# Block products of a feed-forward layer with three accumulator tiles, and token sums dealt out between pieces of a plain tile

## The chip, the cores and the metric

One core of a Trainium2 chip runs the whole kernel. The metric is the device time of one execution in microseconds (us), taken on that core; several executions are timed and their median counts. A profile is one further execution, recorded by the hardware profiler. The engines are named as in the profile: PE is TensorE (matmuls), PEld its weight loads, DVE is VectorE, ACT is ScalarE, POOL is GpSimd, SP issues the DMAs.

## The reference

Two trunk layers over 128 context tokens and 512 latent tokens, 1024 channels. Each layer has a mixer of three branches and a gated feed-forward part of width 2816. The change concerns the feed-forward part of the second layer:

```python
xf = rmsnorm(h, p['norm_ffn'][l]) * (1 + sc_f) + sh_f
gu = xf @ p['ffn_w_in'][l]
h = h + g_f * ((jax.nn.silu(gu[..., :D_FF]) * gu[..., D_FF:]) @ p['ffn_w_out'][l])
```

## The kernel before, in words

All 640 tokens are held with channels on the 128 partitions and tokens along the free axis, in two halves of 320 tokens (`HF`). Every fp32 operand is split into a high part in fp32r (`xh`, `wh`, `ah`) and the rest (`xl`, `wl`, `al`), and each product is three matmuls: high by high, low by high, high by low.

Weights come in tiles of 128 output channels: `fg0` to `fg21` are the gate's columns, `fu0` to `fu21` the up projection's, `fo` the output projection's. A tile's 1024 input channels are loaded in two pieces of 512 (`wr`, three buffers); ACT copies a piece to `wh` (L505, three buffers), and POOL (L509) or, for block products, DVE (L507) subtracts to `wl`. A plain tile is 8 x 2 x 3 = 96 matmuls of 128x320 (`mm_k`, L554), in one accumulator tile of two PSUM banks, one bank for each half of the tokens (`psg`, L428, three buffers). `Stream` (L288) keeps the list of all these units of work; `step` emits one block of input channels, and `ahead` loads and splits the weights of the next units.

In the second layer most gate and up tiles are not plain. `NPL = (22, 2)` (L32) says that of 22 tiles 22 are plain in the first layer and 2 in the second; the other 20 are **pairs**: `fg` and `fu` of the same number, taken as a 2x2 block matrix (gate and up by two halves of the input channels) times the 2x2 blocks of the input (two halves of the channels by two halves of the tokens). Seven products in place of eight give the four result blocks. A product is 4 x 3 = 12 matmuls (`mm_block`, L546). Its weight operand is a block or a sum of blocks (`ws`, on DVE, L534), its input operand a block of `xh`, `xl` or one of the token sums `xeh`, `xel`.

The seven products of a pair add up in one PSUM tile: products 1, 6, 7 and 4 in its bank 0, product 2 in bank 1, and after that products 5 and 3 in bank 1 (`PRODS`, L280; the last entry says whether a product starts a sum). Between them the partial sums are read out: `snap` (L1576, tile `sn`) copies bank 0 after products 1, 6 and 7, on ACT; `c11` (L1588, into `th`) reads bank 1 after product 2, `c22` (L1592, into `su`) after product 5, `c12` (L1595, into `th`) after product 3, and `mul` (L1602, L1603) reads bank 0 after product 4, all on DVE. The products of neighbouring pairs are interleaved: with q the present pair and n the next, the order on PE is q.6, q.5, q.7, n.1, q.4, n.2, q.3, then n.6 and so on. From the first pair on, these instructions keep the order in which they are written (`o`, L486). After each group of tiles (0 to 7, 8 to 14, 15 to 21) the eight output tiles `fo` follow as plain ones.

Ahead of this part stands `join` (L764) with the end of the output projection `wo7`, the norm and the modulated input, and then `token_sums` (L728): for each of four channel blocks k it adds the shift to the tiles `us` of k and k + 4 (ACT, L733, two pieces a tile, 128 and 512 tokens), makes four differences on DVE (L736 into `xt1`, L737 to L739 into `tsum`), copies `tsum` to `xeh` (ACT, L740) and subtracts to `xel` (DVE, L741). The order of these instructions, and of the weight splits written after them, is a scheduler's, by the order in which they are written and by readiness.

Of the kernel before, what the change touches and what calls it, by code (L numbers as in the profile page):

```python
# [18 lines left out]
P = 128  # L19
# [5 lines left out]
HF = T // 2  # L25
# [3 lines left out]
EPS = 1e-6  # L29
QL, KL, RD = 256, 128, 32  # L30
GROUPS = (((0, 11), (11, 22)), ((0, 8), (8, 15), (15, 22)))
NPL = (22, 2)  # L32

O_MQ, O_CKV, O_KR = 0, 256, 384
O_GQ, O_GK, O_GV, O_GR, O_GLR = 416, 672, 928, 1440, 1952
# [248 lines left out]
def mark(s):  # L284
    pass


class Stream:  # L288


    def __init__(self, load, split, psum, mm, mmb, ring):
        self.load, self.split, self.psum, self.mm, self.mmb, self.ring = load, split, psum, mm, mmb, ring
        self.subs, self.units, self.uses = [], [], []
        self.seen = {}
        self.done = set()
        self.posts = {}
        self.ps = {}
        self.raw = {}
        self.w = {}
        self.u = self.k = 0  # L300
        self.debt = 0.0
# [45 lines left out]
    def step(self):  # L347
        u = self.units[self.u]
        name, i, k0, kn, xs, c, last = (u[n] for n in ("name", "i", "k0", "kn", "xs", "c", "last"))
        if self.k == 0:  # L350
            first, then = u["pre"] if isinstance(u["pre"], tuple) else (u["pre"], None)
            if first:
                first()
            self.ahead()
            if then:
                then()
            if name not in self.ps:
                self.ps[name] = self.psum()
        k = self.k
        if u["prod"]:  # L360
            self.mmb(self.ps[name][:, c, :HF], self.w[i], k, xs, u["start"] and k == 0, k == kn - 1)
        else:
            self.mm(self.ps[name], self.w[i], k, k0 + k, xs, k0 + k == 0, last and k == kn - 1, c)
        self.k += 1
        if self.k == kn:
            self.k = 0
            self.u += 1
            self.uses[i] -= 1
            if self.uses[i] == 0:
                del self.w[i]  # L370
            if u["prod"]:
                if last:
                    self.done.add(name)
            elif last and (u["ph"] or c in (None, 1)):
                ps = self.ps[name] if c == 0 else self.ps.pop(name)
                ps = ps[:, :, :HF]
                with self.prio("pp"):
                    if u["ph"]:
                        self.posts[name](ps, c)
                    else:  # L380
                        self.posts.pop(name)(ps)
                if c != 0:
                    self.done.add(name)
                else:
                    self.done.add(name + "/0")
        return 0.82 if c is None else 0.41

    def steps(self, n):
        for _ in range(n):
            self.step()  # L390

    def fill(self, us):
        self.debt += us
        while self.debt > 0 and self.ready():
            self.debt -= self.step()
# [8 lines left out]
def tile_hybrid(ctx: ExitStack, tc, a):  # L404
# [11 lines left out]
    def pool(name, side, bufs=1):  # L416
        return tc.tile_pool(name=name, bufs=bufs, side=side, reuse_waits="tile")
# [10 lines left out]
    def psg(name):  # L428
        return ps2.tile([P, 2, 512], F32, name=name, tag="g")

    def psb(shape, name):
        return ps1.tile(shape, F32, name=name, tag="b")
# [79 lines left out]
    class Pair:  # L512


        def __init__(self, name, top, low):
            self.name, self.t, self.f = name, {}, int(name[2:].split(".")[0])
            self.src = {"A11": top[:, 0:512], "A12": top[:, 512:1024], "A21": low[:, 0:512], "A22": low[:, 512:1024]}
# [196 lines left out]
    def modulate_in(hs, us, rs, sc, sh, c, ds):  # L714
        for d in ds:
            t = us[d]
            if d < 7:
                (ge if OPT["mx"] >> d & 1 else ve).tensor_tensor(t[:, HS[c]], t[:, HS[c]], rs[:, HS[c]], op=ALU.mult)  # L718
            else:
                for i, s, e in PIECES[c]:  # L720
                    ve.scalar_tensor_tensor(t[:, s:e], hs[d][:, s:e], sc[:, d, i:i + 1], rs[:, s:e], op0=ALU.mult, op1=ALU.mult)
            for i, s, e in PIECES[c]:
                se.activation(xh[:, d, s:e], t[:, s:e], AF.Identity, bias=sh[:, d, i:i + 1])  # L723
            for i, s, e in PIECES[c]:
                ve.scalar_tensor_tensor(xl[:, d, s:e], t[:, s:e], sh[:, d, i:i + 1], xh[:, d, s:e], op0=ALU.add,  # L725
                                        op1=ALU.subtract)

    def token_sums(us, sh, xeh, xel, xt1, pool_):  # L728
        h0, h1 = HS
        for k in range(4):  # L730
            for d in (k, k + 4):
                for i, s, e in ((0, 0, TP), (1, TP, T)):
                    se.activation(us[d][:, s:e], us[d][:, s:e], AF.Identity, bias=sh[:, d, i:i + 1])  # L733
            u, v, t1 = us[k], us[k + 4], xt1[:, k]
            t = pool_.tile([P, 3, HF], F32, name="tsum", tag="tsum", bufs=2)
            ve.tensor_tensor(t1, u[:, h1], u[:, h0], op=ALU.subtract)  # L736
            ve.tensor_tensor(t[:, 0], v[:, h1], t1, op=ALU.subtract)  # L737
            ve.tensor_tensor(t[:, 1], v[:, h1], u[:, h1], op=ALU.subtract)
            ve.tensor_tensor(t[:, 2], v[:, h0], t[:, 0], op=ALU.subtract)  # L739
            se.activation(xeh[:, k], t, AF.Copy)  # L740
            ve.tensor_tensor(xel[:, k], t, xeh[:, k], op=ALU.subtract)  # L741
# [7 lines left out]
    def resid_posts(names, hs, g, nm, keep=False):  # L749
        def post(ps, c=None, d=0):  # L750
            if d < 7:
                h_update(hs, d, ps, g)
                nm.add(d, hs[d])
                if keep:
                    dma(hsp[d], hs[d])
            else:
                h_update(hs, d, ps, g, (c,))
                nm.end(hs[d], c)
                if keep:
                    dma(hsp[d][:, HS[c]], hs[d][:, HS[c]])  # L760
        for d in range(8):
            G.posts[names[d]] = lambda ps, c=None, d=d: post(ps, c, d)

    def join(name, hs, nm, after, pre=None):  # L764

        if pre:
            pre()
        G.to(name + "/0")
        G.steps(5)
        nm.fin(0)  # L770
        G.to(name)
        after(0, range(4))
        nm.fin(1)
        after(0, range(4, 8))
        after(1, range(8))
# [101 lines left out]
    def pair_l2(p, B, gp, keep, l):  # L877
        G.to(f"dq{p}.{l}")
        if OPT["l2"] == 0:
            l2_finish(p, ("dk",), B, gp, keep)  # L880
            fill(f"l2a{p}")
        G.to(f"dv{p}.{l}")
        fill(f"l2b{p}")
        l2_finish(p, ("dq",) if OPT["l2"] == 0 else ("dk", "dq"), B, gp, keep)
# [664 lines left out]
    class Blocks:  # L1549
# [21 lines left out]
            ve.tensor_tensor(xl[:, 0:4, h1], self.xt1, xh[:, 0:4, h1], op=ALU.subtract)  # L1571

        def ps(self, q, bank):
            return G.ps[q.name][:, bank, :HF]

        def snap(self, q, i):  # L1576
            t = self.s[q.name, i] = self.sn.tile([P, HF], F32, name="sn", tag="sn", bufs=4)
# [35 lines left out]
    def mm_any(ps, w, kw, kx, xs, start, stop, half):  # L1613
        mm_k(ps, w, kw, kx, cur[xs[0]] if isinstance(xs[0], str) else xs, start, stop, half)

    G = Stream(wload, wsplit, lambda: psg("gm"), mm_any, mm_block, 3)
    G.prio = prio

    def job(name, src, kt, xs, halves=None, ks=None, pre=None):
# [6 lines left out]
    for l in range(L):  # L1626
        def k8(n, halves=None, ks=None, l=l, pre=None):
            job(f"{n}.{l}", a["wall"][l, TILES[n]], 8, xs8, halves, ks, pre)
# [35 lines left out]
        for d in range(8):  # L1664
            k8(f"wo{d}", "post" if d == 7 else None)
        gr, npl = GROUPS[l], NPL[l]
        pairs = {f: Pair(f"ff{f}.{l}", a["wall"][l, TILES[f"fg{f}"]], a["wall"][l, TILES[f"fu{f}"]]) for f in range(npl, NF)}
# [6 lines left out]
        for gi, (f0, f1) in enumerate(gr):  # L1674
# [18 lines left out]
            for i, q in enumerate(qs):  # L1693
                r = qs[i - 1] if i else None
                ahead = (qs[i + 1:] + later + [None, None])[:2]
                n, n2 = ahead
# [25 lines left out]
    def fill(name):  # L1722
        G.fill(FILL[f"{name}@{cur['l']}"])
# [70 lines left out]
    for l in range(L):  # L1794
        prm, mod = prms[l], mods[l]
# [106 lines left out]
        with pool("gt", "right", 2) as gt:  # L1902
# [11 lines left out]
            with pool("zs", "left") as zs:  # L1914
# [6 lines left out]
                with pool("bd", "left") as bd, pool("kp", "left") as kp:  # L1921
# [11 lines left out]
                    for p in range(4):  # L1933
# [3 lines left out]
                        while late and f"br1_7.{l}" in G.done:  # L1937
                            q = late.pop(0)
# [30 lines left out]
        mark(f"normf{l}")  # L1969
        gr, npl = GROUPS[l], NPL[l]  # L1970
        if npl < NF:
            xctx = pool("xe", "left")
            F = Blocks(xctx.__enter__(), hs)
            with pool("us", "left") as up:
                us = [up.tile([P, T], F32, name=f"us{d}") for d in range(8)]
                join(f"wo7.{l}", hs, nm, lambda c, ds: modulate_in(hs, us, nm.acc, mod[:, 32:40], mod[:, 24:32], c, ds),
                     lambda: prescale(us, hs, mod[:, 32:40]))
                token_sums(us, mod[:, 24:32], F.xeh, F.xel, F.xt1, up)
        else:
            with pool("us", "left") as up:  # L1980
                us = [up.tile([P, T], F32, name=f"us{d}") for d in range(7)]
                join(f"wo7.{l}", hs, nm, lambda c, ds: modulate(hs, nm.acc, mod[:, 32:40], mod[:, 24:32], c, ds, us),
                     lambda: prescale(us, hs, mod[:, 32:40]))
# [105 lines left out]
```

## Time and profile before

| | |
|---|---|
| Median of 3 runs | 2898.85 us (2898.72 to 2901.0) |
| The profiled execution's own time | 2900.5 us |
| its span | 2898.7 us |
| mean granted clock of PE in it | 0.967 of full speed |
| PE busy | 2696.4 us (93%) |
| DVE, ACT, POOL busy | 1704.1, 1293.2, 1061.6 us |
| DMA | 317.10 MB, mean 109 GB/s |

How to read it: the profiled execution has its own time; its span is what the trace covers, and a change is summed against that execution. A row of the timeline gives the start from the beginning of the span, the time that it lasts, the engine, the line, the operation, output and inputs by the program's names, and how many equal ones are merged. A bracket at its end is the idle time of the engine before it and what ended that. Matmuls overlap in the pipeline: one lasts about 0.31 us, and the next starts about 0.147 us after it.

### The profile page before, as it was taken

The numbers are of one execution on the slowest core, as the hardware profiler recorded it, in microseconds if no ns is written. First come the engines' busy times: TensorE is split into PE (matmuls) and PEld (weight loads), VectorE is DVE, ScalarE is ACT, GpSimd is POOL, SyncE is SP. The second block draws the span as 40 slices with busy tenths as digits, with TensorE's granted clock in tenths as the row PEclk, the third lists the DMA queues.
The fourth block names the chain that finished last, engine by engine and source line by source line (L and its number), as shares of the span: only waits on it lengthen the run. The fifth ranks groups of instructions, "written<-read, shape, count | busy, mean of one in ns | idle before, by whom it ended". The sixth has DMA issues, their size and how long they took to land. (4 is left out here: it accounts for less than half of the span.)

```text
span 2898.7 us, 49712 instructions
## 1 busy us (share of the span) xinstructions
PE 2696.4 (93%) x19204; PEld 2464.4 (85%) x19204; DVE 1704.1 (59%) x3156; ACT 1293.2 (45%) x2438; POOL 1061.6 (37%) x772
## 2 busy tenths in 40 slices
PE   6889999889999999999999899988999998999998
PEld 4788888778879899999988888876877897898987
DVE  4765584747655699177358576566333336737373
ACT  5575655543333522122366555655233345424244
POOL 3543222333325467366445423233323352020203
PEclk9999999989999999999999999998999998999999
DMA  6254433345434355244323534332434231222222
GB/s 207 90 161 141 91 82 93 91 124 170 140 101 132 104 189 178 84 141 155 109 79 118 178 89 93 77 95 66 136 79 98 63 125 44 81 77 74 77 69 78
DMA packets 291836, 317.10 MB, mean 109 GB/s; under 512 B 163696, under 2 KB 174768, under 8 KB 291472
## 3 DMA queue, kind: packets, MB, share of 16 engines
q1 hardware_dynamic: 291600, 313.92, 37.0%
q8 instruction: 152, 2.49, 0.4%
q14 instruction: 84, 0.69, 0.1%
HBM read 266.01 MB, written 47.82 MB: 108 GB/s over the span
## 5 line engine op out<-in xcount | busy, mean ns | idle before, releaser
L509 POOL TENSOR_TENSOR wl<-wr,wh 128x512 fp32r<-128x512 f32 (+1 forms) x496 | 712.4, 1440 | 1446.4 <-ACT wh L505 1307.2
L554 PE MATMUL gm<-xh,wh 128*128 128x320 f32 x2816 | 700.3, 325 | 30.1 <-ACT xh L704 7.3
L554 PE MATMUL gm<-xl,wh 128*128 128x320 f32 x2816 | 686.4, 319 | 9.1 <-DVE xl L711 4.5
L554 PE MATMUL gm<-xh,wl 128*128 128x320 f32 x2816 | 681.5, 318 | 11.9 <-POOL wl L509 11.9
L505 ACT ACTIVATE wh<-wr 128x512 fp32r<-128x512 f32 (+1 forms) x536 | 331.1, 621 | 697.9 <-PE gm L554 433.1
L554 PEld LDWEIGHTS gm<-xh,wh 128*128 128x128 f32 x2816 | 482.4, 193 | 56.1 <-ACT xh L704 10.6
L554 PEld LDWEIGHTS gm<-xl,wh 128*128 128x128 f32 x2816 | 487.2, 193 | 26.8 <-DVE xl L711 10.3
L554 PEld LDWEIGHTS gm<-xh,wl 128*128 128x128 f32 x2816 | 485.8, 193 | 20.4 <-POOL wl L509 14.1
L629 DVE CUSTOM_DVE_ANT_0 ctb<-wmt,cbb 128x1024 f32<-128x1024 f32 (+1 forms) x200 | 297.5, 1487 | 3.4
L746 DVE SCALAR_TENSOR_TENSOR h<-gm,mod,h 128x128 f32<-128x128 f32 x168 | 63.9, 434 | 250.4 <-PE gm L554 249.8
L554 PE MATMUL gm<-ah,wh 128*128 128x320 f32 x704 | 164.1, 310 | 0.4 <-DVE h L746 0.2
L554 PE MATMUL gm<-ah,wl 128*128 128x320 f32 x704 | 163.4, 309 | 0.5 <-POOL wl L509 0.5
L554 PE MATMUL gm<-al,wh 128*128 128x320 f32 x704 | 163.3, 309 | 0.0
L1071 ACT ACTIVATE VN<-ch 64x64 f32<-64x64 f32 x320 | 69.6, 218 | 176.4 <-DVE vs L1068 162.7
L554 PEld LDWEIGHTS gm<-ah,wh 128*128 128x128 f32 x704 | 118.3, 188 | 1.7 <-DVE h L746 1.4
L554 PEld LDWEIGHTS gm<-ah,wl 128*128 128x128 f32 x704 | 118.4, 188 | 0.8 <-POOL wl L509 0.8
L554 PEld LDWEIGHTS gm<-al,wh 128*128 128x128 f32 x704 | 118.4, 188 | 0.2
L546 PE MATMUL gm<-xh,wh 128*128 128x320 f32 x320 | 101.1, 316 | 11.1 <-ACT sn L1578 11.1
L554 PE MATMUL gm<-ol,wh 128*128 128x320 f32 x384 | 99.9, 334 | 1.6 <-POOL ol L559 1.6
L554 PE MATMUL gm<-oh,wh 128*128 128x320 f32 x384 | 98.9, 334 | 0.6 <-DVE gth L1743 0.3
L546 PE MATMUL gm<-xl,wh 128*128 128x320 f32 x320 | 99.0, 309 | 0.0
L546 PE MATMUL gm<-xh,wl 128*128 128x320 f32 x320 | 98.9, 309 | 0.0
(793 smaller groups left out, 4781.5 us busy)
## 6 DMA issues: line engine op xcount, KB each, us to landing
wr<-in_wall_dram SPq DMA_DIRECT2D x392, 256.0 KB, 2.9
wmt<-in_wmodt_dram SPq DMA_DIRECT2D x60, 512.0 KB, 3.7
wr<-in_wfo_dram SPq DMA_DIRECT2D x64, 256.0 KB, 2.7
wr<-in_wbr_dram SPq DMA_DIRECT2D x48, 256.0 KB, 2.7
wmt<-in_wmodt_dram SPq DMA_DIRECT2D x40, 256.0 KB, 3.2
wq<-in_wall_dram SPq DMA_DIRECT2D x40, 256.0 KB, 2.8
wm<-in_wmod_dram SPq DMA_DIRECT2D x16, 512.0 KB, 8.4
wr<-in_wfo_dram SPq DMA_DIRECT2D x32, 192.0 KB, 2.4
```

What stands on the lines that cost most here:

```text
L505: o(se.activation(wh[:, :w], wr[:, :w], AF.Copy))
L509: ge.tensor_tensor(wl[:, :w], wr[:, :w], wh[:, :w], op=ALU.subtract)
L546: o(pe.matmul(ps, w_[:, wsl], x_[k], start=(start and i == 0), stop=(stop and i == 2), skip_group_check=True))
L554: o(pe.matmul(ps[:, c, :HF], w_[:, wsl], x_[kx][:, c * HF:(c + 1) * HF], start=(start and i == 0), stop=(stop and i == 2)))
L629: ins = ve.tensor_tensor_reduce(self.t, wm, self.c[:, i], 0.5, 0.0, ALU.mult, ALU.add, accum_out=acc[h][:, m - m0, i:i + 1])
L746: o(ve.scalar_tensor_tensor(hs[d][:, s:e], ps[:, c, s - c * HF:e - c * HF], g[:, d, i:i + 1], hs[d][:, s:e], op0=ALU.mult, op1=ALU.add))
L1071: se.activation(VN[d * 64:(d + 1) * 64, h, n], ps[h * 64:(h + 1) * 64, 1], AF.Copy)
```

## The change

Three edits, which belong together:

- The accumulators of a pair are three PSUM tiles: each product that starts a sum (1, 2 and 5) takes a new one by `bank(c)`. For bank 0 that is the first half of a two-bank tile of `psg` (three buffers), for bank 1 a one-bank tile of `psb` (L431, two buffers). `mm_block` and the readers take the tile by name and bank.
- `NPL` becomes (22, 3): tiles 0, 1 and 2 of the second layer are plain, and 19 pairs are left.
- `token_sums` gets the name of the first gate tile, and ahead of each of its four blocks it lets the stream emit up to five steps of that tile (`within`), but not the tile's last step. So the splits that go with these steps are written between the token sums.

```diff
-NPL = (22, 2)
+NPL = (22, 3)
...
             if then:
                 then()
-            if name not in self.ps:
+            if u["prod"] and u["start"]:
+                self.ps.setdefault(name, {})[c] = self.bank(c)
+            elif name not in self.ps:
                 self.ps[name] = self.psum()
         k = self.k
         if u["prod"]:
-            self.mmb(self.ps[name][:, c, :HF], self.w[i], k, xs, u["start"] and k == 0, k == kn - 1)
+            self.mmb(self.ps[name][c], self.w[i], k, xs, u["start"] and k == 0, k == kn - 1)
...
+    def within(self, name, n):
+
+        for _ in range(n):
+            u = self.units[self.u]
+            if u["name"] == name and not (u["last"] and self.k == u["kn"] - 1):
+                self.step()
+
...
-    def token_sums(us, sh, xeh, xel, xt1, pool_):
+    def token_sums(us, sh, xeh, xel, xt1, pool_, name):
         h0, h1 = HS
         for k in range(4):
+            G.within(name, 5)
             for d in (k, k + 4):
...
         def ps(self, q, bank):
-            return G.ps[q.name][:, bank, :HF]
+            return G.ps[q.name][bank]
...
+    def bank(c):
+        return psb([P, 512], "gm")[:, :HF] if c else psg("gm")[:, 0, :HF]
+
+    G = Stream(wload, wsplit, lambda: psg("gm"), bank, mm_any, mm_block, 3)
```

Line numbers in the changed kernel are up to 13 higher than before. Below, rows of the programs' orders before and after; the numbers behind the names tell buffers apart, and a bracket says for which engines' semaphores the instruction has waits.

**PE, second layer, in the third pair: from the last matmul of product 6 to the second block of product 5.** `gm` is the accumulator. Before:

```order
L546 MATMUL gm_24977<-xeh_24230,wh_25012 128x320
L546 MATMUL gm_24977<-xel_24231,wh_25012 128x320
L546 MATMUL gm_24977<-xeh_24230,wl_25013 128x320
L546 MATMUL gm_24977<-xh_98,wh_25041 128x320 [waits Activation_49]
L546 MATMUL gm_24977<-xl_99,wh_25041 128x320
L546 MATMUL gm_24977<-xh_98,wl_25042 128x320 [waits DVE_49]
```

Changed:

```order
L555 MATMUL gm_25108<-xeh_24230,wh_25143 128x320
L555 MATMUL gm_25108<-xel_24231,wh_25143 128x320
L555 MATMUL gm_25108<-xeh_24230,wl_25144 128x320
L555 MATMUL gm_25215<-xh_98,wh_25173 128x320 [waits DVE_49,Activation_49]
L555 MATMUL gm_25215<-xl_99,wh_25173 128x320
L555 MATMUL gm_25215<-xh_98,wl_25174 128x320 [waits DVE_49]
```

Product 5 wrote the same tile as product 6 (bank 1 and bank 0) and has a wait on ACT. Now it writes a tile of its own, and a wait on DVE is added.

**PE, the same pair: from the last matmul of the next pair's product 1 to product 4.** Before:

```order
L546 MATMUL gm_25122<-xh_98,wh_25079 128x320
L546 MATMUL gm_25122<-xl_99,wh_25079 128x320
L546 MATMUL gm_25122<-xh_98,wl_25080 128x320
L546 MATMUL gm_24977<-xeh_24230,wh_25097 128x320 [waits DVE_49,Activation_49]
L546 MATMUL gm_24977<-xel_24231,wh_25097 128x320
L546 MATMUL gm_24977<-xeh_24230,wl_25098 128x320
```

Changed:

```order
L555 MATMUL gm_25255<-xh_98,wh_25211 128x320
L555 MATMUL gm_25255<-xl_99,wh_25211 128x320
L555 MATMUL gm_25255<-xh_98,wl_25212 128x320
L555 MATMUL gm_25108<-xeh_24230,wh_25230 128x320 [waits Activation_49]
L555 MATMUL gm_25108<-xel_24231,wh_25230 128x320
L555 MATMUL gm_25108<-xeh_24230,wl_25231 128x320 [waits DVE_49]
```

Product 4 had waits on DVE and ACT; now ACT alone at its first matmul, and DVE at its third, for the low part of its own weights.

**ACT, second layer, in the token sums.** `us` are the modulated tiles, `xeh` a token sum's high part, `wh` a weight copy: the first `wh` here belongs to the second half of fu0, the other to the first half of fg1. Before:

```order
L733 ACTIVATE us2_24238<-us2_24238,mod1_103 128x512
L740 ACTIVATE xeh_24230<-tsum_24409 128x960 [waits DVE_49]
L733 ACTIVATE us6_24242<-us6_24242,mod1_103 128x128
L733 ACTIVATE us6_24242<-us6_24242,mod1_103 128x512 [waits Activation_49]
L733 ACTIVATE us3_24239<-us3_24239,mod1_103 128x128
L733 ACTIVATE us3_24239<-us3_24239,mod1_103 128x512
L740 ACTIVATE xeh_24230<-tsum_24420 128x960 [waits DVE_49]
L733 ACTIVATE us7_24243<-us7_24243,mod1_103 128x128
L740 ACTIVATE xeh_24230<-tsum_24431 128x960 [waits DVE_49]
L733 ACTIVATE us7_24243<-us7_24243,mod1_103 128x512 [waits Activation_49]
L505 ACTIVATE wh_24507<-wr_24462 128x512 [waits DMAHW5_49,PE_49]
L505 ACTIVATE wh_24552<-wr_24493 128x512 [waits DMAHW6_49,PE_49]
```

Changed:

```order
L743 ACTIVATE us4_24240<-us4_24240,mod1_103 128x512 [waits DVE_49]
L514 ACTIVATE wh_24507<-wr_24405 128x512 [waits DMAHW5_49,PE_49]
L743 ACTIVATE us5_24241<-us5_24241,mod1_103 128x128
L743 ACTIVATE us5_24241<-us5_24241,mod1_103 128x512
L750 ACTIVATE xeh_24230<-tsum_24431 128x960 [waits DVE_49]
L743 ACTIVATE us2_24238<-us2_24238,mod1_103 128x128
L743 ACTIVATE us2_24238<-us2_24238,mod1_103 128x512
L743 ACTIVATE us6_24242<-us6_24242,mod1_103 128x128
L743 ACTIVATE us6_24242<-us6_24242,mod1_103 128x512 [waits Activation_49]
L750 ACTIVATE xeh_24230<-tsum_24448 128x960 [waits DVE_49]
L743 ACTIVATE us3_24239<-us3_24239,mod1_103 128x128
L743 ACTIVATE us3_24239<-us3_24239,mod1_103 128x512
```

The copy of fu0's second half moved from behind all the pieces of `us` to behind the second piece of us4. The copy of fg1's first half still stands behind the third `xeh`, four rows further down than this piece shows.

## Rows read from the trace of the kernel before

**Rows 1.** The page's first part: busy time of each engine.

```profile
PE 2696.4 (93%) x19204; PEld 2464.4 (85%) x19204; DVE 1704.1 (59%) x3156; ACT 1293.2 (45%) x2438; POOL 1061.6 (37%) x772
```

**Rows 2.** The chain of waits in the second feed-forward part: start, length, count.

```profile
2429.38 19.20 PE gm L554 x116
...
2462.09 7.29 PE gm L546 x48
2469.90 5.56 PE gm L546 x36
2475.95 7.29 PE gm L546 x48
...
2536.91 56.32 PE gm L554 x384
```

**Rows 3.** Timeline of PE, ahead of a pair's product 4 and product 5.

```profile
2600.77 0.31 PE L546 MATMUL gm<-xh,wl 128*128 128x320 f32 x1
2601.59 0.38 PE L546 MATMUL gm<-xeh,wh 128*128 128x320 f32 x1 [0.51 <-ACT sn L1578]
...
2608.55 0.31 PE L546 MATMUL gm<-xeh,wl 128*128 128x320 f32 x1
2609.39 0.42 PE L546 MATMUL gm<-xh,wh 128*128 128x320 f32 x1 [0.53 <-ACT sn L1578]
```

**Rows 4.** Timeline of ACT and DVE in the same pair: the readers of the accumulators.

```profile
2601.12 0.44 ACT L1578 ACTIVATE sn<-gm 128x320 f32<-128x320 f32 x1 [0.80 <-PE gm L546]
2608.90 0.44 ACT L1578 ACTIVATE sn<-gm 128x320 f32<-128x320 f32 x1 [0.49 <-PE gm L546]
...
2600.96 0.48 DVE L1592 TENSOR_TENSOR su<-gm,sn 128x320 f32<-128x320 f32 x1
2605.38 0.49 DVE L1588 TENSOR_TENSOR th<-gm,sn 128x320 f32<-128x320 f32 x1 [0.50 <-PE gm L546]
...
2607.14 0.49 DVE L1595 TENSOR_TENSOR th<-gm,sn 128x320 f32<-128x320 f32 x1
```

**Rows 5.** Windows: length, busy PE, PEld, DVE, ACT, POOL; clock, DMA share, GB/s.

```profile
2448.57:2536.91 88.34, 81.02 (x530) 77.52 (x530) 60.08 (x101) 40.47 (x73) 3.03 (x3) 1.00 0.24 73
2593.23:2690.28 97.05, 89.81 (x591) 86.33 (x590) 67.97 (x117) 45.65 (x82) 1.81 (x2) 1.00 0.24 74
2739.56:2835.87 96.31, 89.58 (x590) 86.34 (x590) 63.87 (x110) 44.70 (x80) 3.61 (x3) 1.00 0.22 63
...
2422.27:2434.49 12.22, 6.61 (x28) 6.05 (x27) 8.29 (x14) 8.23 (x13) 5.09 (x3) 0.72 0.23 64
```

**Rows 6.** Timeline of ACT, DVE and POOL around the token sums.

```profile
2418.01 2.52 ACT L733 ACTIVATE us<-us,mod 128x512 f32<-128x512 f32 x5
2420.44 0.99 ACT L740 ACTIVATE xeh<-tsum 128x960 fp32r<-128x960 f32 x1
2426.01 1.13 ACT L505 ACTIVATE wh<-wr 128x512 fp32r<-128x512 f32 x2
...
2442.15 1.15 ACT L505 ACTIVATE wh<-wr 128x512 fp32r<-128x512 f32 x2 [6.36 <-DMA wr<-in_wall_dram]
...
2421.69 1.15 DVE L741 TENSOR_TENSOR xel<-tsum,xeh 128x960 fp32r<-128x960 f32 x1
...
2426.75 2.57 POOL L509 TENSOR_TENSOR wl<-wr,wh 128x512 fp32r<-128x512 f32 x1 [15.37 <-ACT wh L505]
...
2437.97 1.30 POOL L509 TENSOR_TENSOR wl<-wr,wh 128x512 fp32r<-128x512 f32 x1
```

**Rows 7.** Timeline of PE at the second half of tile fu0.

```profile
2421.98 0.46 PE L554 MATMUL gm<-xh,wl 128*128 128x320 f32 x2
2426.67 0.80 PE L554 MATMUL gm<-xh,wh 128*128 128x320 f32 x2 [4.24 <-ACT wh L505]
...
2429.38 0.90 PE L554 MATMUL gm<-xh,wl 128*128 128x320 f32 x2 [1.37 <-POOL wl L509]
```

More of the change, by code (lines that the diff above doesn't have):

```diff
@@ L288, with __init__ @@
 class Stream:
-    def __init__(self, load, split, psum, mm, mmb, ring):
-        self.load, self.split, self.psum, self.mm, self.mmb, self.ring = load, split, psum, mm, mmb, ring
+    def __init__(self, load, split, psum, bank, mm, mmb, ring):
+        self.load, self.split, self.psum, self.bank, self.mm, self.mmb, self.ring = load, split, psum, bank, mm, mmb, ring
         self.subs, self.units, self.uses = [], [], []
@@ L1614, in mm_any @@
         mm_k(ps, w, kw, kx, cur[xs[0]] if isinstance(xs[0], str) else xs, start, stop, half)
-    G = Stream(wload, wsplit, lambda: psg("gm"), mm_any, mm_block, 3)
+    def bank(c):
+        return psb([P, 512], "gm")[:, :HF] if c else psg("gm")[:, 0, :HF]
+    G = Stream(wload, wsplit, lambda: psg("gm"), bank, mm_any, mm_block, 3)
     G.prio = prio
@@ L1977, in tile_hybrid @@
                      lambda: prescale(us, hs, mod[:, 32:40]))
-                token_sums(us, mod[:, 24:32], F.xeh, F.xel, F.xt1, up)
+                token_sums(us, mod[:, 24:32], F.xeh, F.xel, F.xt1, up, f"fg0.{l}")
         else:
```

## Prediction

> **What bounds the kernel now.** I read four views, from the whole to the place. The page's first part [rows 1] says that PE is busy for 93% of the span: what shortens the kernel is PE work that goes, or PE waits that go. The change touches only the second layer's feed-forward part, from about 2399 us on, so I followed the chain of waits there [rows 2]. The reader is to see two rates. A plain stretch runs 384 matmuls in 56.32 us, 146.7 ns each. The block products come in pieces of 36 and 48 matmuls, with a hole between one piece and the next: the piece that starts at 2462.09 is followed by that of 2469.90 and this one by 2475.95, so one pair (7 products of 12, 84 matmuls) takes 13.86 us, where 84 x 0.1467 are 12.32. In the timeline of PE [rows 3] the holes stand before product 4 (the matmul before it starts at 2600.77, so the next could at 2600.92, and does at 2601.59) and before product 5 (2608.70 against 2609.39).
>
> Who ends the holes? The profile names the snapshot `sn` of ScalarE both times [rows 3]. For product 5 that is right: the snapshot of 2608.90 lasts to 2609.34 [rows 4], and product 5 starts 0.05 us later. It reads bank 0, product 5 writes bank 1, but both are one tile. Before product 4 two instructions end together [rows 4]: a snapshot at 2601.56 and the add `su` at 2601.44. That snapshot is of the next pair's tile, which product 4 does not touch; `su` reads bank 1 of the tile whose bank 0 product 4 writes, and the order of PE has a wait on DVE there. So I take `su`, and this hole too is a wait between two halves of one tile.
>
> **The change, part by part.**
>
> *Three accumulators.* No matmul is added or taken. The two waits lose their cause: in the new order product 4 has a wait on ScalarE alone, for its weights and for the snapshot after product 7, which is one whole product (12 matmuls, 1.76 us) back. To sum what goes I take whole stretches [rows 5], with the matmuls counted from the pieces of the chain (the rows count two or three more, which reach over the edges): 88.34 us for 528, so 88.34 - 77.44 = 10.90 us lost; 97.05 for 588, so 97.05 - 86.24 = 10.81; 96.31 for 588 (24 of them plain), so 10.07. Sum 31.78 us over 20 pairs.
>
> What may take their place? Product 5 opens a tile in a pool of two buffers and gains a wait on DVE, for the add that last read the buffer. The candidates (L1588, L1595) end at 2605.87 and 2607.63 [rows 4]; product 5 could start at 2608.70: 1.07 us to spare at worst. Behind a late product 5 stand all later products on PE; ahead of those adds on DVE stand the weights' low parts, which wait for ScalarE's copies; the order has both two products (3.5 us) ahead of their use. With a pair at 12.32 us the load of DVE rises from 67.97 of 97.05 us [rows 5] to 67.97 of 86.24, 79%: not the bound. And the pieces of 48 already run four products without a hole, at the pace that is now wanted throughout. I charge nothing for new waits; the bounds are 0 and 0.2 us a pair, 3.8 us in all (four times the 0.05 us from an awaited end to PE's start).
>
> *Does the clock add anything?* The granted clock is 1.00 in all three stretches [rows 5], and the pieces run at the 147 ns of the plain stretch [rows 2]: the upper of the two levels (2.4 GHz). So a hole costs its length alone. The Trainium skill (TensorE: Matmul & The Clock Gate, section "A second HAM failure mode: psum-queue depth-cycling") says that short idle times between groups of matmuls that cycle through PSUM can make the clock swing between its levels; by that, more than 31.78 us would come back. The trace shows no such swing here, and the sum stays.
>
> *The third plain tile.* A pair of 84 block matmuls (12.32 us without holes) becomes 96 plain ones, 14.08 us: +1.76 us. Its low parts are on POOL, four of 1.30 us [rows 6] beside 14.08 of PE: hidden. The pair's seven low parts and four weight sums leave DVE, off the path. The first pair's two loads now hold two of the three load buffers during the third tile in place of the second; there ScalarE waited 6.36 us for a load [rows 6], but PE ran 116 matmuls in one piece across it [rows 2], so that stays covered.
>
> *Token sums.* PE's order does not change up to the end of tile fu0's first half; what moves is one weight copy `wh` on ScalarE. Before, PE is through with that half at 2421.98 + 0.29 = 2422.27 [rows 7], waits 4.24 us for the copy of the second half, 1.37 for its low part from POOL, and then runs below full clock: 0.72 in this stretch [rows 5]. So 24 matmuls (3.52 us) take 12.22: 8.70 us lost. The copy stood on ScalarE behind all sixteen bias pieces and three `xeh` of the token sums, at 2426.01 [rows 6]. Now it stands behind the second piece of us4, the first of the five that begin at 2418.01 [rows 6]: done at about 2419.3, its low part at 2421.9 at the latest. No wait there.
>
> But the copy for fg1's first half stays behind the token sums. ScalarE then has the pieces of five tiles (about 0.9 us a tile, 4.6) and three `xeh` (0.99 each), and each `xeh` waits for three sums of DVE, between which `xel` (1.15) now stands [rows 6]: by my estimate from these rows the copy comes at 2426.5 and ends at 2427.15, where it was before. PE is through fu0 at 2422.27 + 3.52 = 2425.79 and waits 1.4 us, then for the low part. POOL took 2.57 us for one such part while DVE ran token sums, 1.30 later [rows 6]. With 2.57 the second wait is about 1.7, with 1.30 it is 0.5; the last of the sums still runs on DVE then, so I take 2.57. The Trainium skill (GPSIMD Engine Reference, section "1. Specifications") says that POOL shares its way to SBUF with VectorE and contends with instructions of two SBUF inputs; the two rows agree. Lost after the change: 1.4 + 1.7 = 3.1 us at full clock, and 2.9 more if the other 20 matmuls run at the lower level (1.2 GHz, twice 0.147 us): between 3.1 and 6.0, in the middle 4.5. Gain 8.7 - 4.5 = **4.2 us**; bounds 8.7 (no wait left) and 0 (the same wait, one piece later).
>
> *Sum.* -31.78 + 1.76 - 4.2 = -34.2 us. Against the profiled execution's own 2900.5 us (span 2898.7) that is 2866.3; the median of the runs stands 1.65 lower, at 2898.85: **2864.6 us**, 1.2% faster. With the bounds: 4.5 less if the start loses nothing, 4.2 more if it gains nothing, up to 3.8 more for new waits: 2860.1 to 2872.6, and with the spread of runs (2898.72 to 2901.0) 2858 to 2873.
>
> **The rivals.** A measurement can tell about 0.2% (5.8 us) from no change.
>
> 1. *One hole stays.* If the snapshot that the profile names, and not `su`, ends the hole before product 4, about half of 1.54 us remains in each of 19 pairs, 14.6: 2879.2. For it: the profile's releaser, whose end is nearer to PE's start. Against: it reads another tile. 0.09.
>
> 2. *The change does not do what it says.* If PE waits for the snapshots for another reason than the shared tile, each pair still takes 13.86, and a plain tile in place of a pair costs 0.2: 2898.85 + 0.2 - 4.2 = 2894.9, within 0.2%. Against: product 5 starts a sum of its own and needs nothing of bank 0. 0.04.
>
> 3. *Slower: product 5 waits for its buffer.* With only two buffers, a late add on DVE stops PE in every pair. L1588 ends 2.83 us before product 5 could start; each us beyond costs 19. To be slower than 2904.6 there must be 40 / 19 = 2.1 us of wait in each pair, so that add would have to come 4.9 us later than now. For it: DVE works in order, and its low parts wait for ScalarE. Against: in the pieces of 48 it keeps this pace. 0.03.
>
> **How the numbers follow.** The forecast has 0.84. Faster: the forecast and rival 1, 0.93; same: rival 2, 0.04; slower: rival 3, 0.03. The range is the forecast's own; the three rivals, 0.16 in all, lie outside.
>
> **What would show it.** Right: block products in one piece from group to group in the chain, three block stretches of about 65, 86 and 86 us, no wait of PE for `sn`, and a wait of some 3 us at fg1's first half, none at fu0's second. Wrong: holes of about 0.5 us that remain (rival 1: before product 4 alone; rival 2: both), PE waiting for the adds `th` of DVE before product 5 (rival 3), or the 4.24 us wait merely moved by a piece.

## The result, and the profile after

| | before | changed |
|---|---|---|
| Median of 4 runs each, same chip | 2899.93 us (2898.72 to 2903.12) | 2867.59 us (2862.61 to 2873.0) |
| Ratio | | 0.9887 (95%: 0.9867 to 0.9907) |
| The profiled execution's own time, its span | 2900.5, 2898.7 us | 2866.79, 2865.0 us |

The kernel became 1.1% faster; 2864.6 us had been forecast, and the range holds the result. Of the two profiled executions' spans the difference is 33.7 us; the sum was 34.2.

The page's first part, of the changed kernel (compare [rows 1]): 14.6 us less of busy PE, though it runs 12 matmuls more.

```profile
PE 2681.8 (94%) x19216; PEld 2461.6 (86%) x19216; DVE 1699.1 (59%) x3141; ACT 1290.1 (45%) x2431; POOL 1075.7 (38%) x777
```

The chain of waits of the changed kernel, from the first plain tiles to the end of the blocks (compare [rows 2]):

```profile
2430.80 28.06 PE gm L563 x188
2458.86 65.12 PE gm L555 x444
...
2580.30 86.27 PE gm L555 x588
...
2715.85 79.24 PE gm L555 x540
```

Where there were pieces of 36 and 48 matmuls with holes, there is one piece a group (of the last group's 588 matmuls the line has the first 540): 444 matmuls in 65.12 us are 146.7 ns each, the pace of the plain stretch [rows 2]. The windows of the three block stretches and of the two stretches ahead of them say the same (columns as in [rows 5]):

```profile
2423.56:2430.80 7.24, 4.58 (x30) 4.02 (x28) 7.24 (x11) 6.31 (x10) 4.08 (x2) 1.00 0.12 36
2430.80:2458.86 28.06, 28.06 (x190) 27.83 (x191) 10.83 (x12) 9.05 (x15) 12.65 (x9) 1.00 0.29 94
2458.86:2523.98 65.12, 65.12 (x446) 65.12 (x446) 49.72 (x84) 33.43 (x61) 3.37 (x2) 1.00 0.25 78
2580.30:2666.57 86.27, 86.27 (x590) 86.23 (x590) 67.48 (x117) 45.67 (x82) 1.79 (x1) 1.00 0.27 80
2715.85:2802.13 86.28, 86.28 (x591) 86.25 (x590) 63.37 (x110) 44.69 (x80) 3.62 (x3) 1.00 0.23 71
```

444, 588 and 588 matmuls at 0.1467 us are 65.12, 86.24 and 86.24: 0.07 us is lost in all three, where it was 31.78. PE no longer waits for the snapshots. The view of the tile `sn` names those that do:

```profile
who waited for it (us, times):
  ACT th L1608: 2.5, 2
  POOL wl L518: 1.6, 1
  DVE su L1602: 1.0, 1
```

The start is less simple. PE, ACT, POOL and DVE of the changed kernel around the token sums (compare [rows 6, 7]; the last row is the first weight sum of the first pair):

```profile
2425.98 0.57 PE L563 MATMUL gm<-xh,wl 128*128 128x320 f32 x2 [1.67 <-POOL wl L518]
2430.80 0.56 PE L563 MATMUL gm<-xh,wl 128*128 128x320 f32 x2 [0.99 <-POOL wl L518]
...
2419.38 0.61 ACT L514 ACTIVATE wh<-wr 128x512 fp32r<-128x512 f32 x1
...
2428.30 0.61 ACT L514 ACTIVATE wh<-wr 128x512 fp32r<-128x512 f32 x1
...
2420.12 5.80 POOL L518 TENSOR_TENSOR wl<-wr,wh 128x512 fp32r<-128x512 f32 x1 [7.99 <-ACT wh L514]
2429.04 1.71 POOL L518 TENSOR_TENSOR wl<-wr,wh 128x512 fp32r<-128x512 f32 x1 [3.11 <-ACT wh L514]
...
2420.43 0.48 DVE L749 TENSOR_TENSOR tsum<-us,tsum 128x320 f32<-128x320 f32 x1
2422.04 1.15 DVE L751 TENSOR_TENSOR xel<-tsum,xeh 128x960 fp32r<-128x960 f32 x1
2424.72 2.22 DVE L751 TENSOR_TENSOR xel<-tsum,xeh 128x960 fp32r<-128x960 f32 x1
2429.55 1.55 DVE L749 TENSOR_TENSOR tsum<-us,tsum 128x320 f32<-128x320 f32 x1
...
2440.15 0.69 DVE L543 TENSOR_TENSOR ws<-ws,wr 128x512 f32<-128x512 f32 x1 [5.31 <-DMA wr<-in_wall_dram]
```

The copy for fu0's second half came where the order has it, at 2419.38. But its low part took POOL 5.80 us (2.57 before), so PE waits 1.67 us at fu0's second half after all, and then 0.99 at fg1's first; the clock stays at 1.00. From the start of fu0's second half (2423.56) to the first block product are 35.30 us for 216 matmuls (31.68): 3.6 lost, before 8.7. Ahead of that, from fg0's first matmul on, the changed kernel lost 0.5 us more (19.66 us from 2403.90 to 2423.56, before 19.12 from 2403.15 to 2422.27).

### The profile page after: what moved, and what is told of

Read it like the earlier page. It is cut to its first block, busy times and chain, and to the rows that moved or that the text cites. A ratio compares the mean times of both kernels' runs of the same rounds, so it can differ in the third digit from the quotient of the medians.

```text
span 2865.0 us, 49715 instructions
## 1 busy us (share of the span) xinstructions
PE 2681.8 (94%) x19216; PEld 2461.6 (86%) x19216; DVE 1699.1 (59%) x3141; ACT 1290.1 (45%) x2431; POOL 1075.7 (38%) x777
## 5 line engine op out<-in xcount | busy, mean ns | idle before, releaser
L518 POOL TENSOR_TENSOR wl<-wr,wh 128x512 fp32r<-128x512 f32 (+1 forms) x500 | 723.3, 1450 | 1407.0 <-ACT wh L514 1287.0
L563 PE MATMUL gm<-xh,wh 128*128 128x320 f32 x2848 | 706.2, 324 | 25.6 <-ACT xh L713 7.0
L563 PE MATMUL gm<-oh,wl 128*128 128x320 f32 x384 | 96.1, 326 | 0.0
```

The costliest lines, as they stand in the source:

```text
L518: ge.tensor_tensor(wl[:, :w], wr[:, :w], wh[:, :w], op=ALU.subtract)
L563: o(pe.matmul(ps[:, c, :HF], w_[:, wsl], x_[kx][:, c * HF:(c + 1) * HF], start=(start and i == 0), stop=(stop and i == 2)))
```

## The experiments

For the start, all kernels are measured by the same stretch: from the first matmul of gate tile fg0 behind the norm to the first block product. A gate or an up tile is 8 x 2 x 3 = 48 matmuls, and not the 96 that stand above for a plain tile: 96 are gate and up together, and half a tile is 24. Less 0.1467 us for each of the stretch's 192 (two plain tiles) or 288 matmuls (three), what is left was lost. In the kernel before the stretch begins at 2403.15 and ends at 2448.57: 45.42 - 28.16 = 17.3 us lost, half of it ahead of the change's place. This is read from the traces, since the medians move by 0.2% from run to run. The kernel with the add moved, below, has the start of before and took 46.18 us for it: differences under 0.8 us are not read as an effect. Each kernel has one trace. The ratios are against the kernel before, on the same chip.

| kernel | plain tiles | sums dealt out | stretch | lost |
|---|---|---|---|---|
| before | 2 | no | 45.42 | 17.3 |
| tok_alone | 2 | yes | 44.98 | 16.8 |
| third_alone | 3 | no | 59.62 | 17.4 |
| tok_third | 3 | yes | 54.96 | 12.7 |
| acc_alone | 2 | no | 46.18 | 18.0 |
| acc_tok | 2 | yes | 44.25 | 16.1 |
| acc_third | 3 | no | 59.53 | 17.3 |
| changed | 3 | yes | 54.96 | 12.7 |
| two_tiles | 3 | yes | 54.95 | 12.7 |

The first four have before's accumulator, the others the changed one (two_tiles a variant of it).

**The accumulators alone.** Against the changed kernel:

```diff
-NPL = (22, 3)
+NPL = (22, 2)
...
-            G.within(name, 5)
```

> The three accumulator tiles alone, with two plain tiles first and the token sums in one run as before. Theory (each hole before products 4 and 5 is a wait between two halves of one tile): all holes go, 31.8 us less than before, a ratio of 0.989; the start of the feed-forward part keeps its 4.24 us wait for the weight copy and its half clock, 8.7 us lost. Rival (a good part of the gain of the whole change comes from the token sums): a gain well under 25 us here.

Measured: 2871.15 us, ratio 0.990 (0.9885 to 0.9915). The block stretches are 77.44, 86.28 and 86.28 us. The theory holds: nearly the whole gain is this edit's. Its first two block stretches in the chain, and the start's wait for the copy:

```profile
2455.00 77.44 PE gm L555 x528
...
2588.76 86.28 PE gm L555 x588
...
2432.34 0.90 PE L563 MATMUL gm<-xh,wh 128*128 128x320 f32 x2 [4.90 <-ACT wh L514]
```

**What ends the hole before product 4.** The kernel before, with one add moved:

```diff
-                pre = do(n and ("snap", n, 1), ("c22", q)), do(n and ("sums", n, "S3"), not n and r and ("low", r))
+                pre = do(n and ("snap", n, 1), not n and ("c22", q)), do(n and ("sums", n, "S3"), not n and r and ("low", r))
...
-                    G.product(n, 2, (None, do(r and ("low", r))))
+                    G.product(n, 2, (do(("c22", q)), do(r and ("low", r))))
```

> The kernel before with its one accumulator of two halves; only the add that reads half 1 of the accumulator (into su) is issued on VectorE behind product 4 in place of ahead of it. Theory (product 4 waited for that add, since the program orders it behind the read of the other half): the hole before product 4 goes wherever a next pair follows, that before product 5 stays; pieces of 36 and 48 matmuls become pieces of 84, a pair takes 13.1 us in place of 13.86, and the time is 13 to 15 us less than before. Rival (the snapshot that the profile names ends that hole): the hole stays at 0.5 us, and the time is that of before.

Measured: 2887.78 us, ratio 0.9945 (0.9928 to 0.9961), 14.2 us below the median of before beside it. The chain of waits of this kernel:

```profile
2587.61 12.61 PE gm L546 x84
...
2600.24 0.45 ACT sn L1578
...
2600.72 12.60 PE gm L546 x84
```

One hole a pair is left, the one before product 5, and a pair takes 13.11 us (13.86 before). So the add `su` ended the hole before product 4, though the profile had named the snapshot, whose end lay nearer [rows 3, 4].

**Two tiles in place of three.** Against the changed kernel; product 5 keeps the tile that product 2 opened:

```diff
             if u["prod"] and u["start"]:
-                self.ps.setdefault(name, {})[c] = self.bank(c)
+                if c not in self.ps.setdefault(name, {}):
+                    self.ps[name][c] = self.bank(c)
```

> The changed kernel with two accumulator tiles in place of three: product 5 goes on in the tile of product 2 instead of opening one of its own, while bank 0 stays a tile apart. Theory (what counts is that product 5 and the snapshot no longer share a tile; a third tile is not needed): no holes, the block stretches keep 65.1, 86.3 and 86.3 us, and the time is the changed kernel's within its spread. Rival (product 5 needs a tile of its own, because the add that reads product 2's sum ends late): a hole before product 5 in each pair, up to 0.7 us, and up to 14 us more.

Measured: 2868.92 us, ratio 0.9884 (0.9862 to 0.9905). Windows of its first and its last block stretch:

```profile
2461.41:2526.53 65.12, 65.12 (x447) 65.12 (x446) 49.75 (x84) 33.36 (x61) 3.38 (x2) 1.00 0.25 78
...
2718.41:2804.69 86.28, 86.28 (x591) 86.25 (x590) 63.41 (x110) 44.69 (x80) 3.62 (x3) 1.00 0.24 71
```

No holes. It is enough that the two banks are two tiles.

**The token sums alone.** The kernel before with `within` and its call:

```diff
         for k in range(4):
+            G.within(name, 5)
```

> The token sums dealt out alone, with before's accumulator and two plain tiles. Theory: the holes of the block products stay, 1.54 us a pair and 13.86 us from pair to pair; the start loses 3.6 us in place of 8.7, so about 5 us less than before, 2895. Rival (the wait is only moved by a piece, or the sums come late for the first block product): within 1 us of before.

Measured: 2899.88 us, ratio 0.999 (0.998 to 0.9999): the gain is at the edge of what can be told. The stretch loses 16.8 us, 0.4 less than before in place of 5, which is within the 0.8. So the rival comes nearer, though its reason holds in part only: the wait moved by a piece and grew shorter, but kept the lower clock behind it. Its PE, POOL and DVE:

```profile
2426.95 0.57 PE L561 MATMUL gm<-xh,wh 128*128 128x320 f32 x2 [2.03 <-ACT wh L512]
2430.38 0.90 PE L561 MATMUL gm<-xh,wl 128*128 128x320 f32 x2 [2.58 <-POOL wl L516]
...
2418.06 3.16 POOL L516 TENSOR_TENSOR wl<-wr,wh 128x512 fp32r<-128x512 f32 x1 [7.99 <-ACT wh L512]
2427.02 3.30 POOL L516 TENSOR_TENSOR wl<-wr,wh 128x512 fp32r<-128x512 f32 x1 [5.81 <-ACT wh L512]
...
2426.44 0.68 DVE L541 TENSOR_TENSOR ws<-ws,wr 128x512 f32<-128x512 f32 x1
2427.04 1.15 DVE L749 TENSOR_TENSOR xel<-tsum,xeh 128x960 fp32r<-128x960 f32 x1
```

And the window behind these waits:

```profile
2430.38:2436.39 6.01, 6.01 (x22) 6.01 (x23) 2.05 (x3) 0.63 (x1) 4.01 (x3) 0.50 0.42 131
```

Here no wait is left at fu0's second half: its low part took 3.16 us on POOL, where it took 5.80 in the changed kernel beside the same order of token sums on DVE. The two waits at fg1's first half that the prediction foretold are there: for the copy, and for the low part, which took 3.30 us. They follow one another with 4 matmuls between, and behind them PE runs at 0.50, the lower of its two levels (1.2 GHz), until 2436.39. DVE computes weight sums (`ws`) of the first pair among the token sums; in the changed kernel the first of them comes at 2440.15, behind them all. From fu0's second half to the first block product (2421.23 to 2446.81) 8.0 us are lost.

**The third plain tile alone.** The kernel before:

```diff
-NPL = (22, 2)
+NPL = (22, 3)
```

> Three plain tiles first in the kernel before, nothing else. Theory: a plain tile of 96 matmuls (14.08 us) takes the place of a pair with its holes (13.86 us), so 0.2 us more than before: no difference that the medians can tell. Rival (the third tile gives the weight sums of the first pair, or the token sums, time that they lacked): 3 us or more less than before, and a wait of PE ahead of the first block product that is there before and not here.

Measured: 2902.98 us, ratio 1.0003 (0.9993 to 1.0012); 17.4 us lost, as before. As expected, it buys nothing there.

**All but the third tile.** The changed kernel with `NPL = (22, 2)`:

> The whole change but for the third plain tile: two plain tiles, and ten pairs in place of nine in the first group. Theory: a pair without holes costs 12.32 us and a plain tile 14.08, so 1.8 us less than the changed kernel, about 2865.8; in the trace the first block stretch has 528 matmuls in 77.4 us and PE waits for nothing ahead of it. Rival (the third tile is there because the token sums or the first weight sums come too late for two): a wait of PE of some us ahead of the first block product, and a time no better than the changed kernel's.

Measured: 2865.92 us, ratio 0.9878 (0.9859 to 0.9896). By the medians it equals the changed kernel. By the stretch it does not: 44.25 us, and with the tenth pair (12.32) 56.57, where the changed kernel takes 54.96. The third tile costs 1.76 us of work, and 3.4 us less are lost with it in these two traces: net 1.6 us gained where 1.8 had been charged. The waits that the rival spoke of are there. PE and POOL of this kernel, and the window behind the first wait:

```profile
2422.77 0.90 PE L563 MATMUL gm<-xh,wl 128*128 128x320 f32 x2 [2.87 <-POOL wl L518]
2435.62 0.56 PE L563 MATMUL gm<-xh,wh 128*128 128x320 f32 x2 [0.25 <-ACT wh L514]
...
2440.38 0.56 PE L563 MATMUL gm<-xh,wh 128*128 128x320 f32 x2 [0.21 <-ACT wh L514]
...
2416.92 5.79 POOL L518 TENSOR_TENSOR wl<-wr,wh 128x512 fp32r<-128x512 f32 x1 [8.00 <-PE gm L563]
```

```profile
2422.77:2426.80 4.03, 4.03 (x17) 4.03 (x18) 4.03 (x7) 3.11 (x4) 0.98 (x1) 0.60 0.21 65
```

Not all of the 3.4 us can be put down to the third tile. Up to fg1's first matmul this kernel has lost 12.5 us, the changed one 11.0, with the same order of PE up to there. The low part of fu0's second half took the same time on POOL (5.79 and 5.80), but PE came to it 1.2 us sooner after fg0's first matmul, waited 2.87 us in place of 1.67, and then ran at a clock of 0.60. That is 1.4 of the 3.4; the other 2.0 come behind, as waits for late copies and their low parts.

The copies at 2435.62 and 2440.38 stood behind late loads (ACT idle for 4.78 and 3.54 us, ended by the DMA of `wr`): by the order of the loads the first pair's hold two of the three buffers there; that this is the cause was not tried apart. That the profiled execution is still 1.6 us shorter than the changed kernel's comes from ahead of the stretch, which began at 2400.69 in this kernel and at 2403.90 in the changed one, with the same order of PE up to that place.

**The changed kernel without its part on the token sums.**

```diff
-            G.within(name, 5)
```

> Three accumulator tiles and three plain tiles, token sums in one run as before: the changed kernel without its part on the token sums. Theory (the token sums dealt out bring 4 to 5 us where three plain tiles follow): no holes, but the 4 to 5 us wait for the copy of fu0's second half and the half clock behind it are back; from the gate tile's first matmul to the first block product 59.6 to 60.3 us, of which PE loses 17.4 to 18.0, against 54.96 and 12.7 in the changed kernel; in all 4.7 to 5.3 us more than that, about 2873. Rival (they bring 0.5 us, as alone with two plain tiles): 55.5 us and the changed kernel's time.

Measured: 2873.47 us, ratio 0.9903 (0.9888 to 0.9917); stretch 59.53 us, 17.3 lost. The theory holds: with three tiles the dealing is worth 4.6 us. The wait for the copy is back:

```profile
2427.43 0.71 PE L563 MATMUL gm<-xh,wh 128*128 128x320 f32 x2 [4.19 <-ACT wh L514]
```

**Both parts of the start, without the accumulators.** The kernel before, `NPL = (22, 3)`, and the token sums dealt out:

> Token sums dealt out and three plain tiles, with before's accumulator. Alone the token sums gained 0.5 us (PE lost 16.8 us ahead of the first block product, before 17.3) and the third tile 0 (17.4). Theory (the two need one another: with three tiles PE's waits fall in two shorter ones and the clock stays up, and the accumulators have no part in that): PE loses 12.7 to 13 us there, 54.9 to 55.3 us in all, as in the changed kernel; holes of 1.54 us a pair stay; about 4.5 us less than before. Rival (the dealing is worth 0.5 us whatever follows, and the changed kernel's start came out well by its accumulators): 16.8 us lost, 59 us in all, and the time of before.

Measured: 2896.08 us, ratio 0.9987 (0.9977 to 0.9997). Its chain of waits behind the plain tiles, and its POOL at fg1's first half:

```profile
2453.21 1.77 PE gm L553 x12
2455.01 0.45 ACT sn L1586
```

```profile
2423.40 1.71 POOL L516 TENSOR_TENSOR wl<-wr,wh 128x512 fp32r<-128x512 f32 x1 [3.11 <-ACT wh L512]
```

The stretch begins at 2398.25: 54.96 us, 12.7 lost, just what the changed kernel takes; behind it the holes are back. The two parts need one another, and not the accumulators. Beside tok_alone this is the cleanest view of the third tile: up to fg1's first matmul both have lost 11.0 us, and the 4.1 us between them come at that half tile. There the low part took 1.71 us on POOL here and 3.30 in tok_alone, and the clock stays at 1.00 where it fell to 0.50. In tok_alone weight sums stand among the token sums on DVE at that time, here they do not; that they are what held POOL up was not tried apart.

**The low parts on VectorE.** The changed kernel with two splits moved off POOL:

```diff
-        i = self._sub((name, k0), lambda: self.load(ap), kn)
+        i = self._sub((name, k0), lambda: self.load(ap), kn, "dve" if (name, k0) in (("fu0.1", 4), ("fg1.1", 0)) else None)
```

> The changed kernel with two low parts of weights (tile fu0's second half, fg1's first half) computed on VectorE in place of GpSimd. Theory (the low part took 5.80 us on GpSimd only because VectorE was adding beside it): on VectorE each takes some 0.7 us, PE no longer waits 1.67 us at fu0's second half, and the stretch from there to the first block product, 35.30 us for 216 matmuls in the changed kernel, falls to 32.5 to 33.5: about 2 us less in all. Rival (PE would wait for the token sums or the copies on ScalarE anyway): the wait comes back elsewhere ahead of the first block product and the stretch stays at 35.

Measured: 2868.74 us, ratio 0.9881 (0.9865 to 0.9898). PE and DVE of this kernel:

```profile
2430.34 0.56 PE L563 MATMUL gm<-xh,wh 128*128 128x320 f32 x2 [1.28 <-ACT wh L514]
2432.80 0.56 PE L563 MATMUL gm<-xh,wl 128*128 128x320 f32 x2 [1.61 <-DVE wl L516]
...
2423.23 0.68 DVE L516 TENSOR_TENSOR wl<-wr,wh 128x512 fp32r<-128x512 f32 x1
```

```profile
2432.80:2436.00 3.20, 3.20 (x13) 3.20 (x14) 3.20 (x3) 1.43 (x3) 2.16 (x2) 0.57 0.28 82
```

The part takes 0.68 us and the wait at fu0's second half is gone, as the theory said. The gain is not there: both waits now fall at fg1's first half, one behind the other, and the clock drops to 0.57 behind them. The stretch is 55.89 us, 0.9 longer in place of 2 shorter. The rival is right. The same edit with two plain tiles:

> The same move of two low parts to VectorE, with two plain tiles in place of three. With two tiles and the low parts on GpSimd the stretch from the first matmul of the gate tile to the first block product took 44.25 us, of which PE lost 16.1 us; 4.4 of them in a wait for the low part and the half clock behind it, 2.9 in waits for two late weight loads and their splits. Theory (the loads are fetched when buffers come free, so that they set the end): the first wait goes, those for the loads grow, and the stretch stays at 43 us or more. Rival (the low part alone is to blame): 40.5 us or less, and a total some 5 us below the changed kernel's.

Measured: 2868.07 us, ratio 0.9882 (0.9866 to 0.9897); stretch 42.19 us, 14.0 lost, between what the two expected. The theory's reason fails: PE waits for no load there, only at fg1's first half, 1.18 us for the copy and 2.02 for the low part. So the late loads of acc_tok do not come with two plain tiles as such. With a tenth pair that is 54.51 us, beside 54.96 in the changed kernel, and 14.0 us lost beside 13.6 in low_dve: no difference that these traces could tell. With these two low parts off POOL, then, the third tile gives back nothing that shows.

**The copies earlier.** The changed kernel with a priority of its own for the split of fg1's first half, 70 or 90 in place of 50:

```diff
-        i = self._sub((name, k0), lambda: self.load(ap), kn)
+        i = self._sub((name, k0), lambda: self.load(ap), kn, "early" if (name, k0) == ("fg1.1", 0) else None)
...
-        with prio("pw"):
+        with prio("pe" if lo == "early" else "pw"):
             wh = wp.tile([P, 512], F32R, name="wh", tag="wh")
```

> The changed kernel with the weight copy for fg1's first half moved forward on ScalarE by one token-sum copy and one bias piece. Theory (this copy, at 2428.30 us in the changed kernel, sets PE's second wait): it comes some 1.9 us sooner, its low part is done before PE gets to it, and the stretch from the gate tile's first matmul to the first block product falls from 54.96 to some 53.7 us, 1.2 us less. Rival (the low part on GpSimd, beside the sums on VectorE, takes so much longer that nothing is won, or the wait at fu0's second half grows): 55 us or more.

> The changed kernel with both weight copies (fu0's second half, fg1's first half) one behind the other on ScalarE, ahead of most token sums. The second must wait until PE has left its buffer, about 0.5 us. Theory: as for the move by one place, 53.7 us from the gate tile's first matmul to the first block product, with the 1.67 us wait at fu0's second half the only one left. Rival (ScalarE then stands idle in that wait and the bias pieces behind it come late, so the sums run longer, and so does GpSimd's part beside them): 55 us or more.

Measured: 2868.82 us, ratio 0.9886 (0.9871 to 0.9901), and 2868.01 us, ratio 0.9884 (0.987 to 0.9899). Both theories fall: the stretches are 57.35 and 57.41 us, 2.4 longer. PE and ACT of the first:

```profile
2426.45 0.56 PE L563 MATMUL gm<-xh,wl 128*128 128x320 f32 x2 [1.71 <-POOL wl L518]
2434.05 0.56 PE L563 MATMUL gm<-xh,wh 128*128 128x320 f32 x2 [0.89 <-ACT wh L514]
...
2425.33 0.61 ACT L514 ACTIVATE wh<-wr 128x512 fp32r<-128x512 f32 x1
2432.49 1.00 ACT L750 ACTIVATE xeh<-tsum 128x960 fp32r<-128x960 f32 x1
2433.38 1.66 ACT L514 ACTIVATE wh<-wr 128x512 fp32r<-128x512 f32 x3
```

The moved copy comes at 2425.33, and PE does not wait at fg1's first half. It waits at the second (in the other kernel 3.44 us in one), whose copy still stands behind the last `xeh`; nothing had been charged for that one. None of these versions beats the changed kernel by more than can be told.

## Why the prediction was right, and where not

*The holes*: right, and shown. -31.78 was forecast, 31.78 - 0.07 = 31.71 came. The reading that `su` and not the named snapshot ends the hole before product 4 is shown by the add moved alone. That both holes come from the two banks being one tile is shown by the two-tile kernel. No new wait appeared: product 5's wait on DVE cost nothing visible.

*The clock*: the sum stayed as the rows had it. 31.71 us came back, and the clock was 1.00 in the block stretches before and after. By the Trainium skill (TensorE: Matmul & The Clock Gate, "A second HAM failure mode: psum-queue depth-cycling") more than the 31.78 us could have come back; these traces show no such swing.

*The token sums*: the size was near (4.2 forecast, 8.7 - 3.6 = 5.1 in the stretch named), the working was not, so that is luck. The step "done at about 2419.3, its low part at 2421.9 at the latest. No wait there" failed: the copy started at 2419.38, but POOL took 5.80 us and not the 2.57 of [rows 6], so there was a wait of 1.67. In its place, the 3.1 us said of fg1's first half shrank to 0.99, and the lower clock did not come. So two of the prediction's own signs of being right did not show: no wait at fu0's second half, and some 3 us at fg1's first. The waits that I had described are those of tok_alone: 2.03 and 2.58 us, with half clock behind. But there 8.0 us are lost, more than the 3.1 to 6.0 of the estimate, and the gain is 0.4 us.

*The third plain tile*: the step that failed in kind. "+1.76" for its work is right. That the tile does nothing else is wrong: with the low parts on POOL, the token sums dealt out bring 4.6 us with it (acc_third and third_alone lost 17.3 and 17.4, the changed kernel and tok_third 12.7) and without it 0.4 (tok_alone against the kernel before) or 1.9 (acc_tok against acc_alone). What the traces show beside that is the order on DVE, where the first pair's weight sums leave the token sums, and the low part of fg1's first half in 1.71 us in place of 3.30; that the one causes the other stays open. The sum came out because the two terms were wrong together: -4.2 + 1.76 = -2.4 forecast, and by the stretch 12.7 - 17.3 + 1.76 = -2.8 measured; singly, the sums take 0.4 off the loss and the tile nothing.

*The sum* on the two profiled executions: -31.7 for the holes, +1.76 of work, -4.5 in the start's stretch, +0.75 because that stretch began later (2403.90 against 2403.15) make -33.7, which is the difference of the spans. From fg0's first matmul to the end of the span, which leaves the last term out, the changed kernel is 34.45 us shorter (461.10 against 495.55). That this is so near the 34.2 forecast rests on the holes, which were right, and on the luck of the other two terms.

*The rivals*: none came. Rival 1's price was near: the one hole that the moved add took away was worth 14.2 us, and the rival had 14.6 for the one that stays.

## What to carry to other kernels

Here two banks of one PSUM tile were read and written in turns, and a reader of one bank held up the writer of the other, 1.54 us in each pair: look for such tiles and make the banks separate tiles. Doubt the releaser that a profile names if it reads a tile that the waiting instruction does not touch. Parts of a change that seem to add up should be costed together where they meet on the same engines: here two edits that brought next to nothing alone gave 4.6 us together. Moving one copy forward in ScalarE's full queue only moved the wait to the next one here.

## What was unexpected in the hardware

- **GpSimd beside VectorE.** The same 128x512 subtraction took POOL 1.30 us with DVE idle [rows 6] and 5.80 while DVE ran token sums back to back; in tok_alone it took 3.16 beside the same order of sums. The DVE instruction during which POOL ends is longer as well: in the changed kernel an `xel` took 2.22 us in place of 1.15 and an add 1.55 in place of 0.48, 1.07 more both times, and in tok_alone the first `xel` took 2.26. Why POOL came through at the first `xel` there and at the second in the changed kernel, no run shows. The Trainium skill (GPSIMD Engine Reference, "1. Specifications") speaks of that contention; the sizes are these traces'.
- **The same waiting time can leave the clock up or not.** Waits of 1.67 and 0.99 us with 24 matmuls between them left the clock at 1.00; 1.28 and 1.61 with 4 between were followed by 0.57, and a single wait of 2.87 (acc_tok) by 0.60. So taking the low parts off POOL removed a wait and made the start no shorter.
- **The spread lies ahead of the change.** The first gate tile's matmuls began between 2398.25 and 2409.10 us in the traces of these kernels, 10.85 us apart; runs of the kernel before on one chip lie 11.0 us apart (2896.62 to 2907.62). The stretch behind took 54.95 or 54.96 us in all three kernels with the same start, 45.42 or 46.18 in three with that of before. From the first block product to the end the changed kernel takes 406.1 us and two_tiles 406.2; the three kernels with two plain tiles and the changed accumulators all take 418.5.
